# Rows of a mixed stage transposed in 32 x 32 blocks and stored feature by feature

## The chip, the cores and the metric

The kernel is one program on one core of a Trainium2 chip. Its time is that of the device in microseconds. The engines are TensorE (PE in the profile, its weight loads PEld), VectorE (DVE), ScalarE (ACT), GpSimd (POOL) and SyncE (SP). Every engine works through its own list of instructions in order. SP and ACT also issue DMAs here, and an ACT instruction that stands behind such an issue in the list waits for it.

## The reference

Two layers of a trunk with 256 context rows and 2048 latent rows of 1024 features. Each layer normalises the rows, projects them to 3040 columns, mixes them in three groups of heads and projects the 1024 mixed features back:

```python
y = concat([gated_head_norm(hg_lat, hg_norm_g, hgate),        # gated recurrence, 4 heads
            mla_lat.reshape(B, N, MLA_W) * silu(mgate),       # softmax attention, 4 heads of 128
            gated_head_norm(gla_lat, gla_norm_g, ggate)])     # linear attention, 4 heads
x_new = layer_norm(DEEPNORM_ALPHA * x + gate * (y @ w_out)) * ln_g + ln_b
```

All of it is 32-bit. Products of consequence are split into a high and a low part, so `y @ w_out` is three products (high x high, high x low, low x high).

## The kernel before

There are 18 tiles of 128 rows (2 of context, 16 latent), or 9 pairs of tiles. Each layer has three stages: `project`, `mix`, `output`.

In `mix` two generators are interleaved. `attention` takes one tile after the other and in each two pairs of heads (hp); for one of these it makes the scores (L905 to L909, evacuated by VectorE at L911), the exponential on ScalarE (L921), the transposes of the weights (`ptp`, L947), their split into high and low (`ph` by ScalarE at L79, `pl` by VectorE at L85), the weighted sums (`oc`, L934 and L939), their copy `os` (L963), the last product `poa` (L966) and the scaling into `ym` (L970). In all that is 34 tiles with 68 pairs of heads. `recurrence` walks over the 9 pairs of tiles, first backwards for states alone (`back_states`), then forwards (`recur`): six levels of gated products (`level_scores`, `pa` at L789) whose decays GpSimd multiplies up (tiles `t0` to `t5` at L725, keys and queries at L765), and at the end `chunk_outputs`, which copies the result to `o` (L822), squares it into a tile with the tag `t0` (L825), normalises and gates it on GpSimd (`rrs` L90, L831, L832). It is run 17 times, 9 in the first layer and 8 in the second, whose context is not needed.

Mixed rows go to the DRAM tensor `y` (2304 x 1024): 512 columns of a pair from `chunk_outputs` (L833, one store of 512 KB), 512 of a tile from `attend` (L973, one store of 256 KB), both from SP's queue. The `output` stage loads them by tile (L1074), transposes each of the 8 blocks of 128 x 128 on TensorE (L1081), splits the result out of PSUM (L79, L85) and multiplies it with `w_out` (L1101 to L1103, 48 products of 512 columns a tile).

The order of all instructions on each engine is set when the program is built: a scheduler plays the program through with its own costs and puts what is ready in line, with a bonus for some instructions (`high_priority`). Buffers (tag and `bufs`) bring in the waits. DMAs of both queues take their completion semaphores in turn from one set of eight (DMAHW0 to DMAHW7 in the order below); a DMA waits until the one that had its semaphore before has landed.

Of the kernel before, what the change touches and what calls it, by code (L numbers as in the profile page):

```python
# [7 lines left out]
F32 = mybir.dt.float32  # L8
# [3 lines left out]
ALU = mybir.AluOpType  # L12
# [4 lines left out]
P = 128  # L17
D = 1024
KD = D // P
# [35 lines left out]
class Trunk:  # L55
# [55 lines left out]
    def scratch(self, l):  # L111

        d, c, nt = self.dpool, self.cpool, self.nt
        S = {}
        S["scT"] = c.tile([P, KD, 2], F32, name=f"scT{l}")
        S["shT"] = c.tile([P, KD, 2], F32, name=f"shT{l}")
        S["gate"] = d.tile([2, D], F32, name=f"gate{l}")

        S["F"] = d.tile([P, self.npairs, 2, 3, SEG], F32, name=f"dF{l}")
        S["K"] = d.tile([P, self.npairs, 2, 3, SEG], F32, name=f"dK{l}")  # L120
        S["Q"] = d.tile([P, self.npairs, 3, SEG], F32, name=f"dQ{l}")
        S["nat"] = d.tile([nt, 1536], F32, name=f"dnat{l}")
# [508 lines left out]
    def pair_rows(self, nat, p, c0, c1):  # L631
        return nat[p * SEG:(p + 1) * SEG, c0:c1].rearrange("(j p) n -> p j n", p=P)

    def back_states(self, S, rp, rps):

        nc = self.nc
        st = rp.tile([P, 3, 64], F32, tag="sc", bufs=2, name="stc")
        nc.vector.memset(st, 0.0)
        L3 = 3 * SEG
        ncp = NCT // 2  # L640
        for p in list(range(ncp))[::-1] + list(range(ncp, self.npairs))[::-1]:
            f = rp.tile([P, 1 + L3], F32, tag="fa", name="bf")
            nc.gpsimd.memset(f[:, 0:1], 0.0)
            nc.sync.dma_start(out=f[:, 1:].rearrange("p (b n) -> p b n", b=3), in_=S["F"][:, p, 0])
            k = rp.tile([P, 3, SEG], F32, tag="ka", name="bk")
            nc.sync.dma_start(out=k, in_=S["K"][:, p, 0])
            vt = rp.tile([P, 2, 512], F32, tag="vg", name="bv")
            nc.sync.dma_start(out=vt, in_=self.pair_rows(S["nat"], p, 0, 512))
            pe = rp.tile([P, L3], F32, tag="qa", name="bpe")
            for b in range(3):  # L650
                bs = slice(b * SEG, (b + 1) * SEG)
                nc.vector.tensor_tensor_scan(pe[:, bs], f[:, bs], self.reset, 0.0, op0=ALU.mult, op1=ALU.max)
            tt = rp.tile([P, 3, NCH], F32, tag="btt", bufs=2, name="btt")
            last = [[SEG, 3], [64, NCH]]
            nc.vector.tensor_tensor(tt, view(pe[:], 63, last), view(f[:], 64, last), op=ALU.mult)
            kf = k.rearrange("p b n -> p (b n)")
            nc.gpsimd.tensor_tensor(kf, kf, pe, op=ALU.mult)
            pu = self.chunk_products(rp, rps, k, vt)

            sb = rp.tile([P, NCH, 3, 64], F32, tag="sbt", bufs=2, name="stb")  # L660
            nc.scalar.copy(sb[:, NCH - 1], st)
            for ch in range(NCH)[::-1]:
                to = sb[:, ch - 1] if ch else rp.tile([P, 3, 64], F32, tag="sc", bufs=2, name="stc")
                self.advance(to, sb[:, ch], tt, ch, pu)
            st = to
            nc.sync.dma_start(out=S["sb"][:, p], in_=sb)
            yield 1.0
# [129 lines left out]
    def chunk_outputs(self, S, rp, rps, p, acc, qa, qm, v2, vt, sbt, sts):  # L797
        nc = self.nc
        po = rps.tile([P, 2, 512], F32, tag="R", name="po")
        quads = ((0, 0), (1, 1), (1, 0), (0, 1))  # L800
        for j in range(2):
            for sl in range(4):
                for e, c in quads:
                    rows = slice(64 * e, 64 * e + 64)
                    o = 256 * j + 64 * sl
# [4 lines left out]
        for d, j in ((0, 0), (0, 1), (1, 0), (1, 1)):  # L810
            for sl in range(4):
                for e, c in quads:
                    rows = slice(64 * e, 64 * e + 64)
                    ch, b, o = 2 * j + c, min(sl, 2), 256 * j + 64 * sl
                    tk = slice(64 * ch, 64 * ch + 64)
                    q = qm[sl - 2][rows, d, tk] if sl > 1 else qa[rows, d, sl * SEG + 64 * ch:sl * SEG + 64 * ch + 64]
# [4 lines left out]
        o = rp.tile([P, 2, 512], F32, tag="acc", name="o")  # L821
        nc.scalar.copy(o.rearrange("p j (e n) -> p e j n", e=2), po.rearrange("p e (j n) -> p e j n", j=2))  # L822
        sq = rp.tile([P, 1024], F32, tag="t0", name="sq")
        of = o.rearrange("p j n -> p (j n)")
# [5 lines left out]
        o3 = of.rearrange("p (h d) -> p h d", d=64)  # L830
        nc.gpsimd.tensor_tensor(o3, o3, r.unsqueeze(2).to_broadcast([P, 16, 64]), op=ALU.mult)  # L831
        nc.gpsimd.tensor_tensor(o, o, vt[:, :, 512:1024], op=ALU.mult)  # L832
        nc.sync.dma_start(out=self.pair_rows(S["y"], p, 0, 512), in_=o)  # L833


    def query_group(self, S, ap, aps, t):
# [49 lines left out]
    def attend(self, S, K, ap, aps, G, t, j):  # L886
        nc = self.nc
# [2 lines left out]
        tk = slice(j * P, (j + 1) * P)  # L890
        mg = ap.tile([P, 512], F32, tag="mg", name="mg")
        nc.sync.dma_start(out=mg, in_=S["nat"][t * P:(t + 1) * P, 1024:1536])
        ym = ap.tile([P, 512], F32, tag="ym", name="ym")
        for hp in range(2):
            pexp, rinv = [], []
            for i in range(2):
                h = 2 * hp + i
                sx = ap.tile([P, self.nt], F32, tag="sx", bufs=3, name="sx")
                mx = ap.tile([P, 8], F32, tag="mx", bufs=2, name="mx")
                nb = 0  # L900
                for s in range(0, nk, 512):
                    n = min(512, nk - s)
                    pss = aps.tile([P, 512], F32, tag="s", bufs=2, name="pss")
                    ks = slice(s, s + n)
# [9 lines left out]
                nm = ap.tile([P, 1], F32, tag="nm", bufs=2, name="nm")  # L914
# [5 lines left out]
                sm = ap.tile([P, 1], F32, tag="sm", bufs=4, name="sm")  # L920
                nc.scalar.activation(sx[:, :nk], sx[:, :nk], AF.Exp, bias=nm, accum_out=sm)  # L921
                ri = ap.tile([P, 1], F32, tag="ri", bufs=4, name="ri")
# [19 lines left out]
            high, low = None, None  # L942
            for kc in range(0, nch, 2):
                pt = aps.tile([P, 2, 2, P], F32, tag="pt", bufs=2, name="ptp")
# [3 lines left out]
                ph = ap.tile([P, 2, 256], F32R, tag="ph", bufs=2, name="ph")  # L948
                pl = ap.tile([P, 2, 256], F32R, tag="pl", bufs=3, name="pl")
# [6 lines left out]
                low = (high[0], lastpl) if high is not None else None  # L956
# [7 lines left out]
            po = aps.tile([P, 2, P], F32, tag="mi", name="poa")  # L964
            for i in range(2):
                nc.tensor.matmul(po[:, i, :], os_[:, i * P:(i + 1) * P], S["uv"][:, 2 * hp + i, :],  # L966
                                 start=True, stop=True)
            for i in range(2):
                hs = slice((2 * hp + i) * P, (2 * hp + i + 1) * P)
                nc.vector.scalar_tensor_tensor(out=ym[:, hs], in0=po[:, i, :], scalar=rinv[i], in1=mg[:, hs],  # L970
                                               op0=ALU.mult, op1=ALU.mult)
            yield
        nc.sync.dma_start(out=S["y"][t * P:(t + 1) * P, 512:1024], in_=ym)  # L973

    def mix(self, l, S):

        nc = self.nc
        with ExitStack() as ctx:
            rp = self.pool(ctx)
            ap = Route(lambda: self.pool(ctx), "os mx nm sm ri", "mg", "ym", "ph pl", "cth ctl ks", "cq cqh cql",  # L980
                       "qn ropt ropa ropb", "rh rl", "qh ql", "gap", "cnh cnl", "sx")
            nc.gpsimd.memset(ap.tile([P, 16], F32, name="gap")[:, 0:1], 0.0)
            ps = Route(lambda: self.pool(ctx, psum=True), "mi", "R", "s", "oc", "pt")
            with self.tc.high_priority(offset=self.AHEAD):
                K = {nm: ap.tile([P, self.nt], F32R, name=nm) for nm in ("cth", "ctl", "ks", "cnh", "cnl")}
                src = (S["kT"][:, 0, :], S["kT"][:, 1, :], S["kN"].rearrange("p t n -> p (t n)"))
# [3 lines left out]
                for i in range(3):  # L990
                    if i == 1:
                        G = self.query_group(S, ap, ps, order[0])
                    for s in range(0, self.nt, 512):
                        n = min(512, self.nt - s)
                        ks = slice(s, s + n)
# [46 lines left out]
    def output(self, l, S):  # L1042
        nc, io = self.nc, self.io
        last = l == DEPTH - 1
        with ExitStack() as ctx:
            R = Route(lambda: self.pool(ctx), "yt", "woa", "sto mvo veo rso", "gate", "lng lnb", "z", "xto", "wob", "yhl")
            ps = Route(lambda: self.pool(ctx, psum=True), "low", "pz", "tr")
            nc.vector.memset(ps.tile([P, 512], F32, name="low")[:, 0:1], 0.0)
            gates = {}

# [8 lines left out]
            src = io["w_out"][l].rearrange("(k p) n -> p k n", p=P)  # L1059
            for k in range(KD):  # L1060
                w = R.tile([P, D], F32, tag="yt", bufs=2, name="woraw")
                nc.sync.dma_start(out=w, in_=src[:, k, :])
                for i, ws in enumerate((wh, wl)):
                    tag, n = ("woa", 11) if 2 * k + i < 11 else ("wob", 5)
# [5 lines left out]
            nc.sync.dma_start(out=lnb, in_=io["ln_b"][l:l + 1, :].to_broadcast([P, D]))  # L1070

            def turned(t):
                yt = R.tile([P, D], F32, tag="yt", bufs=2, name="yt")
                nc.sync.dma_start(out=yt, in_=S["y"][t * P:(t + 1) * P, :])  # L1074
                yhl = R.tile([P, 2, KD, P], F32R, tag="yhl", bufs=2, name="yhl")
                yh, yl = yhl[:, 0], yhl[:, 1]
                for q in range(2):
                    pt = ps.tile([P, 4, P], F32, tag="tr", bufs=2, name="pty")
                    for i in range(4):
                        k = 4 * q + i  # L1080
                        nc.tensor.transpose(pt[:, i, :], yt[:, k * P:(k + 1) * P], self.ident)  # L1081
                    self.split(yh[:, 4 * q:4 * q + 4, :], yl[:, 4 * q:4 * q + 4, :], pt)
                return yh, yl

            tiles = list(range(NCT if last else 0, self.ntiles))
# [1 line left out]
            for t in tiles:  # L1087
                yh, yl = nxt
# [8 lines left out]
                for n in range(2):  # L1097
                    cs = slice(n * 512, (n + 1) * 512)
                    pz = ps.tile([P, 512], F32, tag="pz", bufs=2, name="pzo")
                    for k in range(KD):  # L1100
# [5 lines left out]
                                                   op0=ALU.mult, op1=ALU.add)  # L1106
# [6 lines left out]
                dst = io["out"][0][(t - NCT) * P:(t - NCT + 1) * P, :] if last else self.xs_next[rows, :]  # L1113
# [112 lines left out]
```

## Time and profile before

| | |
|---|---|
| median of 2 runs | 3758.14 us (3754.92 to 3761.37) |
| the profiled execution | 3755.9 us, of which its span is 3754.2 us |
| busy: PE, DVE, ACT, POOL | 96%, 57%, 38%, 22% of the span |
| mix stages (not sharply bounded) | about 700 to 1724 us and 2600 to 3560 us |
| output stages | about 1724 to 1930 us and 3560 to 3754 us |
| TensorE clock granted | 0.986 of full speed |

"Busy" is the time in which an engine had an instruction under way; overlapping instructions are counted once. Matmuls overlap, so what one of them costs the queue is the distance between starts in a row, not its own duration. An idle engine costs something only where TensorE waits for it in the end.

### The profile page before, as it was taken

The page shows a single profiled execution, that of the slowest core. Times are in us where ns is not written, and L with a number is a line of the kernel's source. Part 1 is how long each engine was busy: PE and PEld are TensorE (multiplying, and loading weights), DVE is VectorE, ACT ScalarE, POOL GpSimd, SP SyncE. Part 2 cuts the span into 40 slices and gives each one's busy share as a digit, 9 for nine tenths or more (in the row PEclk, how much of TensorE's full clock was granted, in tenths as well). Part 3 has the DMA queues.
Part 4 walks back from the last instruction along what each step waited for, and adds up shares of the span by engine and source line. Part 5 has one row for each costly group of instructions (what it writes and reads, how often), then busy time and mean ns, then how long its engine had stood idle before and what let it go on. Part 6 is the DMA issues. An engine that isn't in the chain of part 4 may idle for free. (4 is left out here: it accounts for less than half of the span.)

```text
span 3754.2 us, 84546 instructions
## 1 busy us (share of the span) xinstructions
PE 3612.3 (96%) x36056; PEld 3264.7 (87%) x36056; DVE 2139.7 (57%) x5026; ACT 1435.5 (38%) x2296; POOL 811.6 (22%) x617
## 2 busy tenths in 40 slices
PE   8999999999999999998999999999999999999999
PEld 5899999888888888887879999998888888888787
DVE  6764242566666666656765442525665566656566
ACT  3525242344444444443115342523443444444400
POOL 1000000001335354341110000000022344644211
PEclk9999999999999999998999999999999999999999
DMA  7774344322122111116435443433221121221342
GB/s 253 234 202 145 126 132 143 111 81 91 49 69 84 56 61 62 55 43 206 153 110 170 146 152 108 154 120 113 83 90 43 60 68 57 78 78 44 102 143 101
DMA packets 263689, 410.79 MB, mean 109 GB/s; under 512 B 39633, under 2 KB 179985, under 8 KB 262289
## 3 DMA queue, kind: packets, MB, share of 16 engines
q1 hardware_dynamic: 261872, 403.04, 33.8%
q8 instruction: 283, 4.64, 0.5%
q10 hardware_dynamic: 1440, 2.36, 0.2%
q14 instruction: 94, 0.76, 0.1%
HBM read 288.66 MB, written 116.67 MB: 108 GB/s over the span
## 5 line engine op out<-in xcount | busy, mean ns | idle before, releaser
L421 PE MATMUL pj<-wh,hl 128*128 128x256 f32 (+1 forms) x2224 | 622.2, 280 | 7.9 <-DVE hl L85 7.9
L421 PE MATMUL pj<-wh,hh 128*128 128x256 f32 (+1 forms) x2224 | 623.9, 281 | 1.7 <-DVE ve L373 1.2
L421 PE MATMUL pj<-wl,hh 128*128 128x256 f32 (+1 forms) x2224 | 622.7, 280 | 0.1
L911 DVE TENSOR_SCALAR_CACHE_REDUCE sx<-pss 128x512 f32<-128x512 f32 (+1 forms) x648 | 402.9, 632 | 206.1 <-PE pss L909 181.7
L85 DVE TENSOR_TENSOR pl<-ptp,ph 128x512 fp32r<-128x512 f32 x580 | 389.5, 687 | 187.5 <-ACT ph L79 184.2
L79 ACT CAST ph<-ptp 128x512 fp32r<-128x512 f32 x580 | 327.9, 586 | 363.7 <-PE ptp L947 358.3
L421 PEld LDWEIGHTS pj<-wh,hl 128*128 128x128 f32 x2224 | 420.1, 189 | 8.7 <-DVE hl L85 8.6
L421 PEld LDWEIGHTS pj<-wh,hh 128*128 128x128 f32 x2224 | 421.1, 189 | 1.8 <-DVE ve L373 1.6
L421 PEld LDWEIGHTS pj<-wl,hh 128*128 128x128 f32 x2224 | 421.0, 189 | 0.6 <-issue 0.6
L947 PE MATMUL ptp<-ident,sx 128*128 128x128 f32 x2320 | 372.9, 279 | 25.4 <-DVE pl L85 15.8
L934 PE MATMUL oc<-ph,cnh 128*128 128x256 f32 x1160 | 339.6, 315 | 22.7 <-ACT ph L79 22.0
L921 ACT ACTIVATE sx<-sx,nm 128x2304 f32<-128x2304 f32 (+1 forms) x136 | 288.4, 2121 | 184.2 <-DVE nm L917 183.7
L432 PE MATMUL pj<-hh,wh 128*128 128x256 f32 x1136 | 317.3, 279 | 0.0
L947 PEld LDWEIGHTS ptp<-ident,sx 128*128 128x128 f32 x2320 | 273.2, 142 | 50.4 <-DVE pl L85 20.2
L432 PE MATMUL pj<-hh,wl 128*128 128x256 f32 x1136 | 316.2, 278 | 0.0
L432 PE MATMUL pj<-hl,wh 128*128 128x256 f32 x1136 | 315.8, 278 | 0.0
L934 PE MATMUL oc<-ph,cnl 128*128 128x256 f32 x1160 | 301.9, 283 | 0.0
L85 DVE TENSOR_TENSOR wl<-wraw,wh 128x1024 fp32r<-128x1024 f32 (+1 forms) x144 | 169.4, 1211 | 230.6 <-ACT wh L79 230.5
L905 PE MATMUL pss<-cth,qh 128*128 128x512 f32 (+1 forms) x648 | 264.9, 409 | 13.7 <-DVE sx L911 13.7
L934 PEld LDWEIGHTS oc<-ph,cnh 128*128 128x128 f32 x1160 | 222.1, 191 | 51.7 <-ACT ph L79 37.9
L939 PE MATMUL oc<-pl,cnh 128*128 128x256 f32 x1160 | 242.9, 291 | 0.0
L906 PE MATMUL pss<-ctl,qh 128*128 128x512 f32 (+1 forms) x648 | 242.9, 375 | 0.0
(253 smaller groups left out, 7888.0 us busy)
## 6 DMA issues: line engine op xcount, KB each, us to landing
wraw<-in_w_in_dram SPq DMA_DIRECT2D x132, 512.0 KB, 4.5
dnat<-stg SPq DMA_DIRECT2D x104, 256.0 KB, 2.1
vg<-dnat SPq DMA_DIRECT2D x17, 1024.0 KB, 6.1
yt<-dy SPq DMA_DIRECT2D x34, 512.0 KB, 3.6
wmt<-in_w_modT_dram SPq DMA_DIRECT2D x64, 256.0 KB, 4.0
fa<-dF SPq DMA_DIRECT2D x18, 768.0 KB, 4.5
ka<-dK SPq DMA_DIRECT2D x18, 768.0 KB, 4.2
dK<-stg SPq DMA_DIRECT2D x36, 256.0 KB, 4.6
```

What stands on the lines that cost most here:

```text
L79: nc.scalar.copy(hi, src)
L85: nc.vector.tensor_tensor(lo, src, hi, op=ALU.subtract)
L421: nc.tensor.matmul(pj[:, j, :n], h[pr][a][:, k, tk], w[b][:, k, :n], start=(k == 0 and a + b == 0), stop=(k == KD - 1 and a == 1))
L432: nc.tensor.matmul(pj[:, j, :], w[b][:, k, cs], h[pr][a][:, k, :], start=(k == 0 and a + b == 0), stop=(k == KD - 1 and b == 1))
L905: nc.tensor.matmul(pss[:, :n], G["qh"][hp][:, i, tk], K["cth"][:, ks], start=True, stop=False)
L906: nc.tensor.matmul(pss[:, :n], G["qh"][hp][:, i, tk], K["ctl"][:, ks], start=False, stop=False)
L911: nc.vector.tensor_scalar(sx[:, ks], pss[:, :n], SCALE, None, op0=ALU.mult, op1=ALU.max, accum_out=mx[:, nb:nb + 1])
L921: nc.scalar.activation(sx[:, :nk], sx[:, :nk], AF.Exp, bias=nm, accum_out=sm)
L934: nc.tensor.matmul(oc, K[k][:, keys(kc, c)], ph[:, c, :], start=(kc + c == 0 and k == "cnh"), stop=False)
L939: nc.tensor.matmul(oc, K["cnh"][:, keys(kc, c)], pl[:, c, :], start=False, stop=(kc + c == nch - 1))
L947: nc.tensor.transpose(pt[:, c, i, :], pexp[i][:, (kc + c) * P:(kc + c + 1) * P], self.ident)
```

## The change

The DRAM tensor becomes `yT`, features by rows (1024 x 2304). In `chunk_outputs` and `attend` VectorE transposes the finished tile in blocks of 32 x 32 (`ot`, 128 x 1024, with the tag `t0` that GpSimd's next level-0 decays use; `yo`, 128 x 256, one for each pair of heads). `put_turned` then writes it with one DMA for each 32 rows, from ScalarE's queue; its runs in DRAM are 32 numbers (128 bytes) long. So a pair of tiles takes 8 DMAs of 512 runs, a pair of heads 4 DMAs of 256 runs: 17 x 8 + 68 x 4 = 408 DMAs in place of 17 + 34 on SP's queue. `output` loads 128 features by 128 rows at a time (runs of 512 bytes, 1024 of them in a tile) and splits this tile directly, with no transposes and no PSUM tile.

```diff
+    def put_turned(self, S, src, f0, n, t0):
+        for a in range(4):
+            dst = S["yT"][f0:f0 + n, t0 + 32 * a:t0 + 32 * a + 32].rearrange("(b f) t -> f b t", f=32)
+            self.nc.scalar.dma_start(out=dst, in_=src[32 * a:32 * a + 32].rearrange("f (b t) -> f b t", t=32))
...
-        nc.sync.dma_start(out=self.pair_rows(S["y"], p, 0, 512), in_=o)
+        ot = rp.tile([P, 1024], F32, tag="t0", name="ot")
+        nc.vector.transpose(out=ot, in_=of)
+        for j in range(2):
+            self.put_turned(S, ot[:, 512 * j:512 * j + 512], 0, 512, (2 * p + j) * P)
...
+            yo = ap.tile([P, 256], F32, tag="yo", name="yo")
+            nc.vector.transpose(out=yo, in_=ym)
+            self.put_turned(S, yo, 512 + 256 * hp, 256, t * P)
             yield
-        nc.sync.dma_start(out=S["y"][t * P:(t + 1) * P, 512:1024], in_=ym)
...
-                yt = R.tile([P, D], F32, tag="yt", bufs=2, name="yt")
-                nc.sync.dma_start(out=yt, in_=S["y"][t * P:(t + 1) * P, :])
+                yt = R.tile([P, KD, P], F32, tag="yt", bufs=2, name="yt")
+                nc.sync.dma_start(out=yt, in_=S["yT"].rearrange("(k p) t -> p k t", p=P)[:, :, t * P:(t + 1) * P])
...
-                    pt = ps.tile([P, 4, P], F32, tag="tr", bufs=2, name="pty")
-                    for i in range(4):
-                        k = 4 * q + i
-                        nc.tensor.transpose(pt[:, i, :], yt[:, k * P:(k + 1) * P], self.ident)
-                    self.split(yh[:, 4 * q:4 * q + 4, :], yl[:, 4 * q:4 * q + 4, :], pt)
+                    ks = slice(4 * q, 4 * q + 4)
+                    self.split(yh[:, ks, :], yl[:, ks, :], yt[:, ks, :])
```

Three places show what the scheduler made of it. The first is ScalarE around the second copy `os` of the first mix stage, with the stores of one pair of heads. Before:

```order
L963 COPY os<-oc 128x256
L921 ACTIVATE sx,sm<-sx,nm 128x2304
L611 COPY kn<-pk 128x384
L79 CAST ph<-ptp 128x512 x2
L611 COPY kn<-pk 128x384
```

Now:

```order
L971 COPY os<-oc 128x256
L638 DMA dy_95<-yo 32x8x32 x4
L611 COPY kn<-pk 128x384
L929 ACTIVATE sx,sm<-sx,nm 128x2304
L611 COPY kn<-pk 128x384
```

Four stores and a copy stand between `os` and the exponential that followed it at once. On TensorE the first transposes of that exponential's result (`ptp`, a row of 6) came after 20 score products of 512 columns behind `poa`; now they come after 25, one group of 256 columns and the products `pu`.

The second is ScalarE around the 14th `os`, with the stores of the first pair of tiles and of a pair of heads. Before:

```order
L963 COPY os<-oc 128x256
L921 ACTIVATE sx,sm<-sx,nm 128x2304
L79 CAST qh<-pq 128x512
L79 CAST ph<-ptp 128x512 x2
L791 COPY acc<-pa 128x1024
```

Now:

```order
L971 COPY os<-oc 128x256
L638 DMA dy_95<-ot 32x16x32 x8
L638 DMA dy_95<-yo 32x8x32 x4
L797 COPY acc<-pa 128x1024
L79 CAST qh<-pq 128x512
L929 ACTIVATE sx,sm<-sx,nm 128x2304 x2
```

Twelve stores, the copy `acc` and a cast stand ahead of the exponentials. On TensorE seven groups of scores, 24 products `pq` and the 32 products `pa` of level 0 now stand between `poa` and the 6 `ptp`, and the `pa` of level 1 come right behind these.

The third is GpSimd at the same place, with what each instruction waits for. `t_12141` and `t_12235` are the level-0 decays `t0` of the next pair. Before:

```order
L725 TENSOR_TENSOR t_12141<-fa 128x768 [waits DVE_49]
L90 TENSOR_TENSOR rrs<-rss,mhalf 128x16 [waits DVE_49]
L725 TENSOR_TENSOR t_12182<-t_12141 128x384 [waits Pool_49]
L831 TENSOR_TENSOR o<-o,rrs 128x1024 [waits Pool_49]
L765 TENSOR_TENSOR ka<-ka,t_12141 128x192x2x2 [waits Activation_49]
```

Now:

```order
L90 TENSOR_TENSOR rrs<-rss,mhalf 128x16 [waits DVE_49]
L837 TENSOR_TENSOR o<-o,rrs 128x1024 [waits Activation_49,Pool_49]
L838 TENSOR_TENSOR o<-o,vg 128x1024 [waits DMAHW2_49,Pool_49]
L731 TENSOR_TENSOR t_12235<-fa 128x768 [waits DMAHW3_49,DMAHW4_49,DMAHW2_49,DMAHW6_49,DMAHW1_49,DMAHW7_49,DMAHW0_49,DVE_49]
L771 TENSOR_TENSOR ka<-ka,t_12235 128x192x2x2 [waits Activation_49,Pool_49]
```

The decays stood ahead of the normalisation; now they stand behind it and wait for VectorE and for the landing of the stores from `ot`, whose buffer they take.

## Rows read from the trace of the kernel before

**Rows 1.** The page: busy us (share of the span) and instructions by engine.
```profile
PE 3612.3 (96%) x36056; PEld 3264.7 (87%) x36056; DVE 2139.7 (57%) x5026; ACT 1435.5 (38%) x2296; POOL 811.6 (22%) x617
```

**Rows 2.** Stretches: us, busy us of PE, PEld, DVE, ACT, POOL; clock, DMA share, GB/s.
```profile
700.00:1724.00 1024.00, 971.77 (x12019) 850.94 (x12018) 647.08 (x1697) 458.25 (x717) 366.55 (x258) 0.98 0.24 75
1724.00:1930.00 206.00, 199.00 (x964) 163.96 (x963) 141.50 (x227) 32.80 (x60) 24.35 (x21) 0.97 0.45 160
2600.00:3560.00 960.00, 924.99 (x11114) 807.17 (x11114) 601.40 (x1574) 431.67 (x663) 331.60 (x235) 0.99 0.22 68
```

**Rows 3.** Timeline of PE: start, us, operation, shapes, count [idle before <-releaser].
```profile
3548.27 1.09 PE L1081 MATMUL pty<-ident,yt 128*128 128x128 f32 x8 [0.54 <-DMA yt<-dy]
```

**Rows 4.** DMA issues: count, KB each, median us to landing.
```profile
v<-dnat SPq DMA_DIRECT2D x34, 256.0 KB, 4.1
...
dy<-ym SPq DMA_DIRECT2D x34, 256.0 KB, 2.1
```

**Rows 5.** Issue on the queue by line: count, ns min/median/max, first and last start.
```profile
L833 SPq DMA_DIRECT2D dy<-o x17: 359/370/526, 1039.3 to 3508.9; - x17
...
L693 SPq DMA_DIRECT2D v<-dnat x34: 579/613/1862, 703.4 to 3428.4; - x34
...
L997 ACTq DMA_DIRECT2D kraw<-dkT x10: 326/326/338, 557.6 to 2436.9; - x10
...
L194 SPq DMA_DIRECT2D gate<-mc x2: 378/734/1089, 111.2 to 111.6; - x2
```

**Rows 6.** Line L194's landings, and all packets from 241.5 to 254 us.
```profile
DMA to landing us min/median/max: 12.5/12.6/12.8
...
DMA packets 1618, 0.57 MB, mean 46 GB/s; under 512 B 1228, under 2 KB 1490, under 8 KB 1618
```

**Rows 7.** Waits: who for whom, us in total, times, longest.
```profile
ACT sx L921 <- DVE nm L917: 183.7, 100, 4.8
```

**Rows 8.** DVE by line and shape: busy us, mean ns | idle before <-releaser.
```profile
L793 DVE COPY_PREDICATED acc<-mask,pa 128x1024 f32<-128x1024 uint8 x102 | 137.0, 1343 | 73.8 <-PE pa L789 67.1 <-issue 5.7
...
L375 DVE TENSOR_SCALAR xt<-xt,mv,rs 128x1024 f32<-128x1024 f32 x36 | 29.1, 809 | 11.6 <-POOL rs L90 11.6
```

**Rows 9.** Timelines of ACT, DVE and PE around the second `os`.
```profile
772.63 0.37 ACT L963 COPY os<-oc 128x256 f32<-128x256 f32 x1 [3.58 <-PE oc L939]
774.71 2.22 ACT L921 ACTIVATE sx<-sx,nm 128x2304 f32<-128x2304 f32 x1 [1.70 <-DVE nm L917]
776.92 0.46 ACT L611 COPY kn<-pk 128x384 f32<-128x384 f32 x1
...
773.81 0.61 DVE L970 SCALAR_TENSOR_TENSOR ym<-poa,ri,mg 128x128 f32<-128x128 f32 x2
...
773.13 0.64 PE L966 MATMUL poa<-uv,os 128*128 128x128 f32 x4
773.53 0.48 PE L905 MATMUL pss<-cth,qh 128*128 128x512 f32 x1
...
778.53 0.82 PE L947 MATMUL ptp<-ident,sx 128*128 128x128 f32 x6
```

**Rows 10.** Timelines of POOL, DVE, ACT and PE around the 14th `os`.
```profile
1026.72 1.47 POOL L725 TENSOR_TENSOR t<-fa 128x768 f32<-128x768 f32 x1
1028.14 2.91 POOL L90 TENSOR_TENSOR rrs<-rss,mhalf 128x16 f32<-128x16 f32 x1
...
1034.23 2.22 POOL L765 TENSOR_TENSOR ka<-ka,t 128x768 f32<-128x768 f32 x1 [0.52 <-ACT km L755]
...
1036.87 2.39 POOL L832 TENSOR_TENSOR o<-o,vg 128x1024 f32<-128x1024 f32 x1
...
1051.53 2.36 POOL L765 TENSOR_TENSOR qa<-qa,fa 128x384 f32<-128x384 f32 x2 [11.31 <-PE pa L789]
...
1045.08 1.03 ACT L791 COPY acc<-pa 128x1024 f32<-128x1024 f32 x1
...
1037.09 0.64 PE L966 MATMUL poa<-uv,os 128*128 128x128 f32 x4
1043.53 0.82 PE L947 MATMUL ptp<-ident,sx 128*128 128x128 f32 x6
```

More of the change, by code (lines that the diff above doesn't have):

```diff
@@ L126, in scratch @@
         S["sb"] = d.tile([P, self.npairs, NCH, 3, 64], F32, name=f"dsb{l}")
-        S["y"] = d.tile([nt, D], F32, name=f"dy{l}")
+        S["yT"] = d.tile([D, nt], F32, name=f"dy{l}")
         return S
@@ L892, in attend @@
         nc.sync.dma_start(out=mg, in_=S["nat"][t * P:(t + 1) * P, 1024:1536])
-        ym = ap.tile([P, 512], F32, tag="ym", name="ym")
         for hp in range(2):
@@ L967, in attend @@
                                  start=True, stop=True)
+            ym = ap.tile([P, 256], F32, tag="ym", name="ym")
             for i in range(2):
                 hs = slice((2 * hp + i) * P, (2 * hp + i + 1) * P)
-                nc.vector.scalar_tensor_tensor(out=ym[:, hs], in0=po[:, i, :], scalar=rinv[i], in1=mg[:, hs],
-                                               op0=ALU.mult, op1=ALU.mult)
+                nc.vector.scalar_tensor_tensor(out=ym[:, i * P:(i + 1) * P], in0=po[:, i, :], scalar=rinv[i],
+                                               in1=mg[:, hs], op0=ALU.mult, op1=ALU.mult)
+            yo = ap.tile([P, 256], F32, tag="yo", name="yo")
+            nc.vector.transpose(out=yo, in_=ym)
+            self.put_turned(S, yo, 512 + 256 * hp, 256, t * P)
             yield
-        nc.sync.dma_start(out=S["y"][t * P:(t + 1) * P, 512:1024], in_=ym)
     def mix(self, l, S):
@@ L979, in mix @@
             rp = self.pool(ctx)
-            ap = Route(lambda: self.pool(ctx), "os mx nm sm ri", "mg", "ym", "ph pl", "cth ctl ks", "cq cqh cql",
+            ap = Route(lambda: self.pool(ctx), "os mx nm sm ri", "mg", "ym yo", "ph pl", "cth ctl ks", "cq cqh cql",
                        "qn ropt ropa ropb", "rh rl", "qh ql", "gap", "cnh cnl", "sx")
@@ L1046, in output @@
             R = Route(lambda: self.pool(ctx), "yt", "woa", "sto mvo veo rso", "gate", "lng lnb", "z", "xto", "wob", "yhl")
-            ps = Route(lambda: self.pool(ctx, psum=True), "low", "pz", "tr")
+            ps = Route(lambda: self.pool(ctx, psum=True), "low", "pz")
             nc.vector.memset(ps.tile([P, 512], F32, name="low")[:, 0:1], 0.0)
```

## The prediction

> **What bounds the kernel.** I read the page first, then a table of stretches, then the waits, then timelines of two places in the mix stage. The page shows TensorE busy for 3612 of 3754.2 us [rows 1], so all its idle time is 142 us. The stretches say the same of each stage: in the two mix stages TensorE idles 52 of 1024 and 35 of 960 us, while ScalarE has 458 and 432 us of work there; in the first output stage it idles 7 of 206 us [rows 2]. So time is won only by work taken from TensorE's list, and lost by whatever makes its list wait. The waits show how ScalarE lies beside it: a hundred times it waited for VectorE ahead of an exponential, 184 us in all, 1.8 us each [rows 7]. That is slack, but little of it at a time.
>
> **Taken away.** TensorE loses 34 x 8 = 272 transposes. A row of eight takes 1.09 us [rows 3]; with some 0.27 us for the last one to drain that is 0.117 us of the queue for each. 272 x 0.117 = 32 us, all of it on the path, since in the output stages TensorE waits for next to nothing. That stage then has 48 products a tile; VectorE has 141 of 206 us there [rows 2], so nothing else takes over. SP loses 51 stores and the waits ahead of them; no wait of TensorE hung on them: 0.
>
> **Added and hidden.** VectorE transposes 17 x [128 x 1024] and 68 x [128 x 256]. The trace has no such operation. Others over 1024 numbers take 0.81 to 1.34 us [rows 8]; I take 1.2, and 0.4 for the small one (two operations of 128 columns took 0.61 us [rows 9]). That is 48 us beside 1248 us of work in 1984 us: hidden, except where a chain below runs through it. The split reads SBUF now: 0, hidden by the products of the tile before. The loads of `yt` become 1024 runs of 512 bytes; they are issued a tile ahead, more than 10 us: 0.
>
> **Added on ScalarE's list.** 408 issues. On that queue an issue of a plain pattern took 0.33 us; on SP the old store of `o` took 0.37 and the load `v`, with 64 partitions, 0.61 [rows 5]. The new stores have 32 partitions and three dimensions. I take 0.5, between 0.36 and 0.61: 204 us (147 to 249) on an engine with 890 us of work in 1984. There is room, so the question is what stands behind each burst.
>
> One pair of heads (51 of the 68 stand without an `ot` burst). From the start of `poa`, T: `ym` ends at T+1.3 [rows 9], the small transpose at about T+1.9, four issues at T+3.3 to T+4.3, `kn` 0.46, the exponential 2.2 and its sum 0.2: T+6.2 to T+7.2. Before, the exponential began 1.6 us after T and its transposes came at T+5.4. The new order puts about 7.6 us of products between (25 score products at the 0.23 us of the rows, one group at half, the rest 1.2 us), so `ptp` stands at T+7.8: covered, with about 1 us over. But this work was taken from places where it covered other waits. Lower bound 0, upper bound 1 us; I take 0.5: 25 us.
>
> A pair of tiles (17). `o` is ready by 1034, ahead of `poa` at 1037.1 = T, because `t0` and the decays no longer stand between [rows 10]. VectorE transposes it by T+1.9. Eight issues end at T+4.8 to T+6.8, four more at T+6.2 to T+9.2, `acc` 1.0 [rows 10], a cast 0.6, the exponential 2.4: T+10.2 to T+13.2. TensorE reaches `ptp` at about T+11.5 (seven groups 7.5, `pq` 2.8, `pa` 0.7): a stall of 0 to 1.7 us. **The longer chain is GpSimd's.** `t0` must wait until the last store from `ot` has landed, 2.1 to 4.1 us after its issue if it goes like the stores and loads of [rows 4]: T+6.9 to T+10.9. Then `t0` 1.5, keys 2.2, queries 2.4 [rows 10], about 6.1 us: T+13 to T+17. The `pa` of level 1 stand at T+12.2 in TensorE's list, so it waits 1 to 5 us. Together 1 to 5.4 us a pair of tiles. Which end it is hangs on how fast runs of 128 bytes go out: 512 in a store are 32 for each of 16 engines. If a run took 25 ns, a store took 0.8 us, the eighth landed at about T+10.4, and the wait was 4.3. I take 4: 68 us. Nothing in the trace excludes that the new order gains a little elsewhere; I put it at 0.
>
> SP's loads take semaphores from the same eight, so after a burst of twelve the next ones wait for its landing, up to some 4 us. They fill buffers a stage ahead: 0, and counted in the upper bounds.
>
> **Sum.** -32 + 25 + 68 = +61 us on the profiled execution's 3755.9 us (span 3754.2 and 1.7 around it): 3817. The median of the two runs is 2.2 us higher, which makes **3819 us**, 1.6% above. A measurement of this kernel tells about 2% (75 us) from no change, so this is "within 2%", close to its edge.
>
> **The rivals.**
>
> *The cover holds.* The scheduler put work ahead of each place where TensorE would have waited. If its costs fit, all stalls are at their lower bounds (17 x 1 us or less) and the 32 us stay: 3726 to 3745. For it: TensorE idles only 87 us in both mix stages now, under the same scheduler. Against it: GpSimd's new wait. Chance 0.16.
>
> *The bursts at their upper bounds.* 17 x 5.4 + 51 x 1 - 32 = +111: about 3869 (3833 to 3900). It decides from 4.9 us a pair of tiles at 0.5 a pair of heads. Chance 0.23.
>
> *Short runs jam the memory.* The only stores of short runs in the trace are 4 bytes long: 1024 of them landed after 12.5 us, and in a stretch of 12.5 us after another such store the queues moved 0.57 MB, though they had more to do [rows 6]. That is 195 ns a run for each engine. If runs of 128 bytes took 50 ns, a store would take 1.6 us, the eighth would land at T+16.7 and level 1 wait until T+22.8, 10.6 us late: 17 x 10.6 + 25 - 32 = +173, 3931. At 100 ns it is 12.8 us more for each, +391, 4149. Against it: the 4-byte runs all fall into the same few kilobytes, these do not, and a store of rows lands in 2.1 us [rows 4]. It makes the kernel slower by more than 2% from about 30 ns a run. Chance 0.20.
>
> The Trainium skill (DMA: Bandwidth & Descriptors, Specifications) gives 512 bytes as the least transfer at full rate; below it the engine reads, modifies and writes. By that rule this rival is the forecast. The trace agrees for 4 bytes, by the 12.5 us above; for 128 bytes no row shows it.
>
> *The transposes cost more than their distance.* One lasts 0.27 us from start to end. If that whole time fell away, 272 x 0.27 = 73 us less, and stalls near 0 would make it 3685, faster by just 2%. Against it: the row of eight in 1.09 us. Chance 0.03. The Trainium skill (VectorE: DVE Perf Modes, The three transpose paths) puts a transpose of 128 x 128 on TensorE at 390 ns, for a 16-bit type. By that the gain would be 106 us, an estimate from that page; the row of eight disagrees, and the sum goes by the row.
>
> That the change does not do what it says (loads of `yt` that wait for all stores, for instance) has no chance of its own: in the new order the first products of the output stage still stand ahead of the last `poa`.
>
> **Numbers.** Forecast 0.38 (3780 to 3833), cover 0.16, bursts 0.23, jam 0.20, more than the distance 0.03. Faster 0.03; within 2%, 0.38 + 0.16 = 0.54; slower 0.23 + 0.20 = 0.43. The range goes from 3724, the cover with nothing lost, to 3940, the jam at 50 ns; outside lie the 0.03 and about half of the jam, 0.13 in all.
>
> **What the profile of the changed kernel would show.** Right: no `pty`; ScalarE's queue with 408 more issues of 0.36 to 0.61 us; output stages some 16 us shorter each; GpSimd's `t0` waiting for stores from `ot`, and TensorE idle ahead of `pa` by 1 to 5 us once a pair of tiles; stores from `ot` landing in under 5 us. Wrong: TensorE idle ahead of `ptp` or the scores in every pair of heads (the price of the small burst is off), landings of 8 us and more (the jam), or mix stages no longer than before (the cover).

## The result, and the profile after

The changed kernel takes 3860.7 us (median of 2 runs, 3860.15 to 3861.26) against 3758.14: ratio 1.029, 95% interval 1.0268 to 1.0312. It is slower by 2.9%. Differences below are given in us as the ratio's distance from 1 times 3750, since the kernel before stood between 3748 and 3758 us beside the different runs: the change is +109 by that measure.

The page after, busy time by engine; its span is 3858.4 us [rows 1]:

```profile
PE 3633.9 (94%) x35784; PEld 3256.4 (84%) x35784; DVE 2168.5 (56%) x5111; ACT 1438.9 (37%) x2296; POOL 811.0 (21%) x617
```

The 272 transposes are gone from TensorE's count. Its idle time rose from 142 to 224.5 us, and its busy time rose too, by 21.6 us. Nobody else became the bound: VectorE got 29 us more, ScalarE 3. By stage (columns as in [rows 2]; the stages now end later, and the third window lies as far behind the last projection product and ahead of the last `poa` as the third of [rows 2], since these moved from 2568.8 to 2626.7 and from 3562.5 to 3670.5 us):

```profile
700.00:1785.00 1085.00, 995.97 (x12009) 855.88 (x12008) 660.01 (x1738) 456.39 (x714) 365.57 (x258) 0.98 0.26 71
1785.00:1990.00 205.00, 190.39 (x869) 155.56 (x869) 143.85 (x231) 35.77 (x64) 26.72 (x21) 0.95 0.50 161
2658.00:3668.00 1010.00, 949.25 (x11105) 819.93 (x11106) 614.54 (x1611) 433.24 (x664) 330.54 (x235) 0.98 0.24 65
```

The two mixes grew by about 61 and 50 us, and TensorE idles 89 and 61 us in them (52 and 35 before). In some 205 us of the first output stage it now does 869 instructions instead of 964, at 0.95 of the clock. From the last `poa` to the last product an output stage takes 211 us instead of 216 and 179 instead of 183.

What TensorE waited for, before and now (who for whom, us, times, longest):

```profile
PE oc L934 <- ACT ph L79: 22.0, 40, 1.8
PE ptp L947 <- ACT sx L921: 8.9, 6, 3.8
PE pzo L1101 <- DVE z L1104: 6.0, 1, 6.0
PE pa L789 <- POOL qa L765: 1.3, 3, 0.7
```

```profile
PE oc L942 <- ACT ph L79: 43.2, 47, 4.1
PE ptp L955 <- ACT sx L929: 24.2, 11, 9.0
PE pzo L1109 <- DVE z L1112: 24.2, 2, 14.2
PE pa L795 <- POOL qa L771: 9.0, 13, 2.0
```

What ScalarE makes late, the casts `ph` and the exponential `sx`, costs most. The products of the output stages (`pzo`) wait for VectorE, which still works off the mix. GpSimd's late queries are a small row.

The new stores on ScalarE's queue (count, ns min/median/max of one issue) [rows 5]:

```profile
L638 ACTq DMA_DIRECT2D dy<-yo x272: 309/462/1624, 750.5 to 3674.3; - x136
L638 ACTq DMA_DIRECT2D dy<-ot x136: 309/520/3125, 1049.6 to 3610.6; - x136
```

Their landings (KB each, median us) [rows 4]:

```profile
dy<-yo ACTq DMA_DIRECT2D x272, 32.0 KB, 1.7
dy<-ot ACTq DMA_DIRECT2D x136, 64.0 KB, 4.4
```

The new transposes on VectorE [rows 8]:

```profile
L982 DVE STREAM_TRANSPOSE yo<-ym x68: 401/445/456, 750.1 to 3671.4; 128x256 f32<-128x256 f32 x68
L840 DVE STREAM_TRANSPOSE ot<-o x17: 1234/1245/1247, 1048.3 to 3605.7; 128x1024 f32<-128x1024 f32 x17
```

Durations are as foretold. Now the waits (who for whom, us, times, longest) of ScalarE and GpSimd [rows 7]:

```profile
ACT sx L929 <- DVE nm L925: 86.0, 52, 6.5
ACT kn L611 <- DMA dy<-yo: 77.1, 16, 6.8
ACT acc L797 <- DMA dy<-ot: 59.2, 7, 11.0
ACT acc L797 <- DMA dy<-yo: 37.4, 4, 9.8
ACT sx L929 <- DMA dy<-yo: 26.7, 7, 10.4
...
POOL t L731 <- DMA dy<-yo: 96.5, 10, 10.7
POOL t L731 <- DMA dy<-ot: 41.2, 4, 11.5
```

A wait of ScalarE "for" a store here is its own list: the instruction stands behind the issues. With four smaller rows that are not shown these come to 241 us at 42 places; ScalarE's old slack ahead of the exponential went from 184 to 86 us. GpSimd's first product of a pair (`t0`, L731) waits 138 us at 14 places.

One such place, the end of a pair of tiles (timelines of ACT, POOL and PE: start, us, operation [idle before <-releaser]) [rows 10]:

```profile
1395.78 0.37 ACT L971 COPY os<-oc 128x256 f32<-128x256 f32 x1 [3.59 <-PE oc L947]
1397.43 5.17 ACTq L638 DMA_DIRECT2D dy<-ot  x8
1402.70 1.98 ACTq L638 DMA_DIRECT2D dy<-yo  x4
1404.72 1.01 ACT L797 COPY acc<-pa 128x1024 f32<-128x1024 f32 x1 [8.57 <-DMA dy<-yo]
1405.63 2.22 ACT L929 ACTIVATE sx<-sx,nm 128x2304 f32<-128x2304 f32 x1
...
1392.96 2.40 POOL L838 TENSOR_TENSOR o<-o,vg 128x1024 f32<-128x1024 f32 x1
1404.89 1.47 POOL L731 TENSOR_TENSOR t<-fa 128x768 f32<-128x768 f32 x1 [9.54 <-DMA dy<-yo]
...
1405.79 2.35 PE L795 MATMUL pa<-qa,km 64*64 64x64 f32 x64 [0.90 <-ACT acc L797]
1408.07 0.44 PE L955 MATMUL ptp<-ident,sx 128*128 128x128 f32 x2
```

From 1397.4 to 1404.7 ScalarE does nothing but issue twelve stores. The copy `acc`, which frees the PSUM tile of `pa`, and the exponential that TensorE's next transposes need both stand behind them; GpSimd starts 2.3 us after the last of the eight `ot` issues. TensorE lives on products in hand until 1404.9 and then thins out: busy 3.16 of the 5 us after 1405, 3.51 of the next 5, with the clock at 0.59 (between 1.2 and 2.4 GHz) where it had been at 1.00:

```profile
1405.00:1410.00 5.00, 3.16 (x70) 2.69 (x70) 1.49 (x2) 5.00 (x5) 4.92 (x4) 1.00 0.05 10
1410.00:1415.00 5.00, 3.51 (x52) 3.17 (x56) 1.45 (x3) 1.92 (x6) 4.70 (x7) 0.59 0.46 136
1415.00:1420.00 5.00, 5.00 (x67) 4.65 (x60) 2.72 (x3) 2.10 (x4) 3.83 (x2) 0.72 0.06 24
```

The small burst at the place of [rows 9] does no harm:

```profile
776.55 0.64 PE L974 MATMUL poa<-uv,os 128*128 128x128 f32 x4
784.89 0.81 PE L955 MATMUL ptp<-ident,sx 128*128 128x128 f32 x6
...
777.87 0.45 DVE L982 STREAM_TRANSPOSE yo<-ym 128x256 f32<-128x256 f32 x1
778.35 1.82 ACTq L638 DMA_DIRECT2D dy<-yo  x4
780.21 0.48 ACT L611 COPY kn<-pk 128x384 f32<-128x384 f32 x1 [3.79 <-DVE sx L919]
780.59 2.22 ACT L929 ACTIVATE sx<-sx,nm 128x2304 f32<-128x2304 f32 x1
```

The exponential ends 6.3 us after `poa` began, `ptp` comes at 8.3, with no idle time ahead of it.

### The profile page after: what moved, and what is told of

It reads as the page before. It is cut to its first block, busy times and chain, and to the rows that moved or that the text cites. A ratio compares the mean times of both kernels' runs of the same rounds, so it can differ in the third digit from the quotient of the medians.

```text
span 3858.4 us, 84719 instructions
## 1 busy us (share of the span) xinstructions
PE 3633.9 (94%) x35784; PEld 3256.4 (84%) x35784; DVE 2168.5 (56%) x5111; ACT 1438.9 (37%) x2296; POOL 811.0 (21%) x617
## 3 DMA queue, kind: packets, MB, share of 16 engines
q10 hardware_dynamic: 147232, 20.21, 3.1%
## 5 line engine op out<-in xcount | busy, mean ns | idle before, releaser
L955 PE MATMUL ptp<-ident,sx 128*128 128x128 f32 x2320 | 372.0, 280 | 48.3 <-ACT sx L929 24.2
L942 PE MATMUL oc<-ph,cnh 128*128 128x256 f32 x1160 | 341.9, 318 | 44.8 <-ACT ph L79 43.2
L795 PEld LDWEIGHTS pa<-qa,km 64*64 64x64 f32 (+1 forms) x6528 | 191.2, 139 | 62.5 <-issue 17.2
```

The lines of the kernel that those rows point to most:

```text
L795: nc.tensor.matmul(out, w, mv, start=True, stop=True, tile_position=pos)
L942: nc.tensor.matmul(oc, K[k][:, keys(kc, c)], ph[:, c, :], start=(kc + c == 0 and k == "cnh"), stop=False)
L955: nc.tensor.transpose(pt[:, c, i, :], pexp[i][:, (kc + c) * P:(kc + c + 1) * P], self.ident)
```

## The experiments

Each ratio is to the kernel before, run beside it; us as above. The scheduler lines up the instructions of each version anew, so an edit brings its own order along: behind the 14th `os`, for example, ScalarE's list in e3 has `acc`, an exponential and `qh`, where the change has twelve stores, `acc`, `qh` and two exponentials. No run holds the order fixed, so each difference is that of an edit together with its order.

| run | median us | ratio (95%) | us |
|---|---|---|---|
| the change | 3860.7 | 1.0290 (1.0268 to 1.0312) | +109 |
| e1_output_only | 3733.6 | 0.9964 (0.9952 to 0.9975) | -14 |
| e2_mix_only | 3882.1 | 1.0362 (1.0340 to 1.0384) | +136 |
| e3_sp_queue | 3769.3 | 1.0060 (1.0043 to 1.0078) | +22 |
| e4_long_runs | 3840.3 | 1.0253 (1.0232 to 1.0274) | +95 |
| e5_long_one | 3810.8 | 1.0160 (1.0144 to 1.0176) | +60 |
| e6_own_ot | 3844.1 | 1.0242 (1.0227 to 1.0257) | +91 |
| e7_sp_long | 3782.5 | 1.0080 (1.0063 to 1.0097) | +30 |
| e8_block_load | 3765.4 | 1.0026 (1.0013 to 1.0039) | +10 |
| e9_output_clean | 3733.1 | 0.9951 (0.9934 to 0.9968) | -18 |
| e10_turns_clean | 3775.2 | 1.0054 (1.0038 to 1.0071) | +20 |
| e11_block_load4 | 3726.0 | 0.9921 (0.9902 to 0.9940) | -30 |
| e12_turns_own | 3745.2 | 0.9989 (0.9979 to 0.9999) | -4 |

### Which half, and which queue

**e1_output_only**

> The output stages alone: the mix stores rows as the kernel before does (one SyncE store for a pair of tiles, one for a tile, 2 KB runs, no VectorE transposes), into the memory that the output stages then read as if it were turned, so the values are those of other places. My prediction put -32 us on this part (272 transposes by 0.117 us): 3726 us, ratio 0.991. If the spare transposes were hidden behind something else, or TensorE's clock eats the gain, 3745 to 3760; if each cost its latency, 3685. If the whole loss of the change lies in the mix, this kernel plus the loss of the mix alone must add up to the changed kernel (+102.6 us).

```diff
+    def ynat(self, S, h):
+        a, n = S["yT"][:, :], self.nt - S["off"]
+        return bass.AP(a.tensor, a.offset + 512 * h * n, [[512, n], [1, 512]])
...
-        nc.vector.transpose(out=ot, in_=of)
-        for j in range(2):
-            self.put_turned(S, ot[:, 512 * j:512 * j + 512], 0, 512, (2 * p + j) * P)
+        nc.sync.dma_start(out=self.ynat(S, 0)[p * SEG - S["off"]:(p + 1) * SEG - S["off"]].rearrange("(j p) n -> p j n", p=P), in_=o)
```

-14 us. But the trace shows TensorE waiting 26.6 us (2 times) ahead of `pzo` for tile loads that could start only after the last store, which the change itself does not have. So the run doesn't settle the size; e9 was made for that.

**e2_mix_only**

> The mix of the changed kernel (VectorE transposes, 408 stores from ScalarE's queue, 128-byte runs), with TensorE's transposes back in the output stages, which read the same memory as natural rows. If the sum holds with -32 us for the output stages: 3860.7 + 32 = 3893 us (ratio 1.036). If the output stages gained nothing: 3861. If the turned loads of the output stages, not the mix, made the loss: 3760 to 3790.

```diff
-                nc.sync.dma_start(out=yt, in_=S["yT"].rearrange("(k p) t -> p k t", p=P)[:, :, t * P:(t + 1) * P])
+                for h in range(2):
+                    nc.sync.dma_start(out=yt[:, 512 * h:512 * h + 512], in_=self.ynat(S, h)[t * P - S["off"]:(t + 1) * P - S["off"]])
...
+                        nc.tensor.transpose(pt[:, i, :], yt[:, k * P:(k + 1) * P], self.ident)
```

The output stages are those of the kernel before, reading `yT`'s memory as rows; the values they read belong to other places. +136: the whole loss is in the mix. Against the change the spare transposes are worth 27 us here.

**e3_sp_queue**

> The same 408 stores issued from SyncE instead of ScalarE; all else as in the changed kernel. Theory 1 (ScalarE's list is held by the bursts of issues, 408 times about 0.5 us and their waits, and what it owes TensorE comes late): most of the loss goes, 3735 to 3790. Theory 2 (the buffer that GpSimd shares with ot comes free only when the last store has landed): little changes, 3840 to 3865. Theory 3 (128-byte runs hold up the DMA engines or the memory for everybody): unchanged, 3850 to 3870. A rival against moving them: SyncE's loads stand behind the stores and come late, 3870 to 3950.

```diff
-            self.nc.scalar.dma_start(out=dst, in_=src[32 * a:32 * a + 32].rearrange("f (b t) -> f b t", t=32))
+            self.nc.sync.dma_start(out=dst, in_=src[32 * a:32 * a + 32].rearrange("f (b t) -> f b t", t=32))
```

+22, so one word takes away 86 of 109 us. The page's line by engine, and the stores' issue by SP:

```profile
PE 3598.6 (96%) x35784; PEld 3237.5 (86%) x35784; DVE 2166.5 (58%) x5111; ACT 1438.3 (38%) x2296; POOL 811.2 (22%) x617
```

```profile
L638 SPq DMA_DIRECT2D dy<-yo x272: 302/443/2147, 750.3 to 3586.2; - x136
L638 SPq DMA_DIRECT2D dy<-ot x136: 303/499/2266, 1037.3 to 3532.4; - x136
```

An issue costs SP as much as ScalarE (0.44 and 0.50 us), but nobody computes there: TensorE's idle time falls from 224.5 to 168.8 us (3767.4 - 3598.6), its busy time by 35 us. Theory 1 holds for most of the loss. The Trainium skill (DMA: Bandwidth & Descriptors, Rules for kernel authors) says that spreading DMAs over queues saves only the sequencer's issue time; here taking the 408 issues off ScalarE's list was worth 86 us.

**e4_long_runs**

> As many stores (408), from ScalarE's queue, with the same bytes and the same 32 partitions each, but every row of a partition is one run of 1 or 2 KB at its natural place (so the values land elsewhere); 8 to 16 times fewer pieces. Theory 1 with a price that does not hang on the pieces: 3850 to 3870. Theory 3, or theory 1 with an issue whose price hangs on the pieces: 3740 to 3800. Theory 2: the landings of ot get shorter with fewer pieces, so 3800 to 3840.

```diff
-            dst = S["yT"][f0:f0 + n, t0 + 32 * a:t0 + 32 * a + 32].rearrange("(b f) t -> f b t", f=32)
-            self.nc.scalar.dma_start(out=dst, in_=src[32 * a:32 * a + 32].rearrange("f (b t) -> f b t", t=32))
+            dst = self.ynat(S, f0 // 512)[t0 - S["off"] + 32 * a:t0 - S["off"] + 32 * a + 32, f0 % 512:f0 % 512 + n]
+            self.nc.scalar.dma_start(out=dst, in_=src[32 * a:32 * a + 32])
```

+95, that is 14 less than the change; the intervals touch. `ot` stores land after 3.5 us instead of 4.4. But e4 has the flaw of e1 too: TensorE waits 17.3 us ahead of `pzo` for tile loads, while its wait for `z` there is 9.4 us, against 24.2 in the change. How much of the 17 us is lost is not settled, so the short runs are worth 14 to some 31 us on ScalarE's queue: a small part either way.

**e5_long_one**

> ScalarE's queue again, natural places as in the run with long runs, but one store of 128 partitions for each yo (68) and two for each ot (34): 102 issues instead of 408, the same bytes, the same VectorE transposes and waits. Theory 1a (each issue's own time holds ScalarE's list, about 0.5 us each): of the 71 us between the 408 long-run stores on ScalarE (3840) and SyncE's version (3769) a quarter stays, 3770 to 3795. Theory 1b (ScalarE's list is held by what the first store of a burst waits for, VectorE's transpose or an old landing, which one store waits for as well): 3820 to 3845.

```diff
+        self.nc.scalar.dma_start(out=self.ynat(S, f0 // 512)[t0 - S["off"]:t0 - S["off"] + P, f0 % 512:f0 % 512 + n], in_=src)
```

+60, 35 less than e4 (both with the 17.3 us ahead of `pzo`) for 306 issues less, about 0.11 us each. Neither band was hit: it fell between 1a and 1b. ScalarE's waits behind stores are down to 9 us, but `t0` waits longer than in e7, where SP issues the same stores (109.1 us, 13 times, against 77.2, 11 times; `ot` lands after 6.2 us against 5.5), so e5 minus e7 is no clean price of an issue.

### The buffer and VectorE's transposes

**e6_own_ot**

> The changed kernel, with ot in the buffer of v2 (read for the last time by TensorE just before, and filled for the next pair of tiles by a SyncE load that has the whole pair's time) instead of that of t0 and sq, so that GpSimd's first product of the next pair no longer waits for the last landing of an ot store. Theory 2 (that wait is the larger term, as my prediction had it: 17 times 4 us = 68 us): 3780 to 3815. Theory 1 (ScalarE's list, whose own next instructions are as late): 3840 to 3865. A rival: SyncE's queue now waits for the landing and the loads behind it come late, 3860 to 3880.

```diff
-        ot = rp.tile([P, 1024], F32, tag="t0", name="ot")
+        ot = rp.tile([P, NCH, 256], F32, tag="v2", name="ot").rearrange("p c n -> p (c n)")
```

+91, 18 less than the change. All waits of `t0` for stores are gone, 138 us of them, and one eighth of that came back. With ScalarE's list held, `acc` and the exponential are late anyway.

**e7_sp_long**

> The VectorE transposes of the changed kernel, with 102 natural stores from SyncE: the mix of before plus 85 transposes, and output stages without TensorE's. Theory 4 (VectorE's 68 times 0.45 and 17 times 1.25 us, about 52 us, lie on the path): 3760 to 3790. My prediction's term (hidden): as the output stages alone, 3730 to 3745.

```diff
-        self.nc.scalar.dma_start(out=self.ynat(S, f0 // 512)[t0 - S["off"]:t0 - S["off"] + P, f0 % 512:f0 % 512 + n], in_=src)
+        self.nc.sync.dma_start(out=self.ynat(S, f0 // 512)[t0 - S["off"]:t0 - S["off"] + P, f0 % 512:f0 % 512 + n], in_=src)
```

The minus line is that of e5. +30; in it TensorE waited 16.2 us for a first tile load, the flaw of e1, so e10 repeats it without.

**e9_output_clean**

> The output stages alone again, without what disturbed the first such run (there each output stage began with 11 to 16 us in which TensorE waited for a tile load that could not start before the last store of the mix): the mix and its stores are the kernel before's, and the output stages load tiles in the changed kernel's pattern (8 runs of 512 bytes to a partition) from a tensor written long before, so their values are others'. My prediction's term: -32 us. From the first run, -13.5 and the 26.6 us of those waits taken off: -40. If the spare transposes were covered: 0 to -15.

```diff
-                nc.sync.dma_start(out=yt, in_=S["yT"].rearrange("(k p) t -> p k t", p=P)[:, :, t * P:(t + 1) * P])
+                nc.sync.dma_start(out=yt, in_=view(S["F"][:, 0, 0, 0, :], t * P, [[12 * P, KD], [1, P]]))
```

The minus line is that of the change; all else is the kernel before, without TensorE's transposes. -18 us (-12 to -25), less than both numbers expected, though TensorE's busy time fell by 24.9 us (to 3587.4). In each output stage `pzo` waits once for VectorE's `z`, 16.1 us in all, against 6.0 before: the products now start while VectorE still works off the mix (the change waits 24.2 us there). That this wait holds the rest of the 32 us is read from the trace, not tested by itself; e11, which has no such wait, gains 30.

**e10_turns_clean**

> As the last, with the VectorE transposes of the changed kernel in the mix, and 102 stores of whole tiles from SyncE (2 and 1 KB runs, natural places); against the last run it shows what the 85 transposes and the waits tied to them cost without ScalarE's queue and without short runs. Theory 4 (VectorE's time, 52 us, lies on the path in the mix): 40 to 55 us above the last run. My prediction (hidden): 0 to 10 us above it. Between: part of them, where a softmax waits behind them on VectorE.

To the load of e9 comes, in `put_turned`:

```diff
+        self.nc.sync.dma_start(out=S["y"][t0:t0 + P, f0:f0 + n], in_=src)
```

+20, so 39 above e9, at the edge of theory 4's band. But its waits name another cause:

```profile
POOL t L729 <- DMA dy<-ot: 76.6, 11, 8.4
PE pa L793 <- POOL qa L769: 22.8, 17, 4.4
ACT acc L795 <- DVE ot L838: 24.6, 12, 4.6
```

`t0` waits for the landing of the `ot` stores, GpSimd's queries come late and `pa` waits for them: the chain of my prediction, seen without ScalarE's bursts.

**e12_turns_own**

> The run with the turns alone (85 VectorE transposes, stores of whole tiles from SyncE, 1.0054), and ot in v2's buffer, as in the run on the changed kernel: GpSimd's first product of a pair of tiles no longer waits for the landing of the store of ot (76.6 us of such waits in the profile of the turns alone, which TensorE sees as waits of pa for qa), while VectorE does the same 52 us of transposes at the same places. Theory 2: most of the 39 us between the turns alone (1.0054) and the output stages alone (0.9951) goes, 0.996 to 0.999. Theory 4 (VectorE's own time on the path): 1.004 to 1.006.

The edit is that of e6, made in e10. -4: of the 39 us 24 went with the buffer, and 14 (4 to 24) are left for all of VectorE's 51 us and the waits tied to it. `t0` no longer waits for any store, and:

```profile
PE pa L793 <- POOL qa L769: 1.0, 2, 0.7
ACT acc L795 <- DVE ot L838: 7.8, 7, 3.1
```

Theory 2 explains most of e10, theory 4 a small rest. Without e12 the 39 us would have been put down to VectorE, because 51 us of transposes look like so good a fit.

The buffer also sets GpSimd's order. In the change, e3 and e10 the next pair's decays stand behind the normalisation at all 15 places where a next pair follows; in e6 and e12 they stand ahead of it again, as before. The first such place in e12:

```profile
1021.54 1.46 POOL L729 TENSOR_TENSOR t<-fa 128x768 f32<-128x768 f32 x1
1022.97 2.90 POOL L90 TENSOR_TENSOR rrs<-rss,mhalf 128x16 f32<-128x16 f32 x1
```

So the 24 us are the price of the shared buffer, the later place in the list and the wait for the landing together; the runs do not part the two.

### A version that beats both

**e8_block_load**

> A version pointed to by these runs: the mix exactly as before (natural stores by SyncE, no transposes there), and the turning in the output stages: each tile's rows are loaded in four crosswise pieces (SyncE, 1 KB runs, 32 partitions each; the order of features over K chunks is another, and w_out's rows are loaded in the same order), VectorE transposes 32x32 blocks once per tile (1.25 us, 34 tiles, 42 us in all) and no TensorE transposes. Nothing is stored in short runs and ScalarE's list holds nothing more. If VectorE's transposes hide in the output stages: 3730 to 3740. If they come before the products of z on VectorE and TensorE waits: up to 42 us more, 3740 to 3780.

```diff
+                for q in range(4):
+                    nc.sync.dma_start(out=yb[32 * q:32 * q + 32].rearrange("u a k f -> u a (k f)"),
+                                      in_=S["y"][t * P:(t + 1) * P, 256 * q:256 * q + 256].rearrange("(a u) n -> u a n", u=32))
+                yt = R.tile([P, 4, KD, 32], F32, tag="ytt", name="yt")
+                nc.vector.transpose(out=yt.rearrange("p a k u -> p (a k u)"), in_=yb.rearrange("p a k f -> p (a k f)"))
...
-            src = io["w_out"][l].rearrange("(k p) n -> p k n", p=P)
+            src = io["w_out"][l].rearrange("(q k f) n -> k q f n", q=4, f=32)
```

+10, no gain, and the cause was neither of the two expected: the end of the mix grew, since ScalarE waited 47.8 us for the new loads of `w_out` (`woraw`; 11.8 us before) with a softmax in line behind.

**e11_block_load4**

> The version that turns tiles in the output stages, with w_out's rows loaded by four plain loads of 32 rows to a chunk instead of one load over rows in four places. In the run before this one the six loads of w_out at the end of a mix were issued over 30 us, in the kernel before over 18, and ScalarE, which copies them, held the last softmax back. If that was its loss: 3705 to 3735. If the loss is VectorE's 34 transposes in the output stages: 3750 to 3770 as there.

```diff
-                nc.sync.dma_start(out=w, in_=src[k])
+                for q in range(4):
+                    nc.sync.dma_start(out=w[32 * q:32 * q + 32], in_=src[k, q])
```

The minus line is that of e8. -30 us (-22 to -37): 0.8% faster than the kernel before and 3.6% faster than the change, the fastest kernel here. Who waited for the loads of `w_out`, in e8 and in e11, and the first output stage of e11:

```profile
  ACT wo L79: 47.8, 14
```

```profile
  ACT wo L79: 23.5, 13
```

```profile
1724.00:1930.00 206.00, 204.48 (x936) 167.27 (x936) 167.37 (x260) 33.60 (x61) 29.21 (x23) 0.99 0.51 161
```

VectorE turns the 34 tiles in the output stages (1.23 us each) and still has 39 us to spare in this stretch, while TensorE idles 1.5 us (7 before).

## Why the prediction was right in part

The range held the time; the likeliest case, "within 2%", did not come. The sum of the runs, each part against its neighbour: outputs -18 (e9), `ot` in `t0`'s buffer +24 (e10 to e12), VectorE and the rest of the new chain +14 (e12 to e9), short runs, 306 more stores on SP and tile loads that again depend on the stores +2 (e10 to e3), ScalarE's queue +86 (e3 to the change): +108. Mine was +61.

- **Bound and stages**: right that TensorE's list decides; no other engine became the bound. But of the 104 us that the span grew 83 are idle time and 22 busy time, where the sum had 32 us less of it. Busy time that grows behind stalls was a term that it did not have.
- **-32 us for the transposes**: the mechanism right, the size too large for this order of work: -18 in e9, -27 between e2 and the change, -30 in e11. The distance in a row is nearer than the whole duration; the output stages did not get 16 us shorter each in the change but 5 and 4, and in them TensorE waits 24.2 us for `z` amid the mix's leftovers. The rival "the transposes cost more than their distance" is refuted: no run gives 73 us. The Trainium skill's 390 ns (VectorE: DVE Perf Modes, The three transpose paths), given for a 16-bit type, would be 106 us, an estimate; the measurement decides against it here: 18 to 30 us by 272 are 0.07 to 0.11 us each.
- **VectorE's transposes hidden**: durations right (1.245 and 0.445 us for 1.2 and 0.4 taken), the 0 nearly right: some 14 us (4 to 24) with the waits tied to them, of which `acc` waiting for `ot` is the part that the trace names.
- **`yt` loads and SP at 0**: right. Loads land after 4.6 us and held ScalarE 5.6 us in all.
- **+25 us for the bursts on ScalarE**: this step failed. The price of an issue was right (0.46 and 0.52 us for 0.5), and the burst that I followed ran as I wrote. What failed is "51 of the 68 stand without an `ot` burst", priced by one exponential at one place: behind a burst stand whatever copies the scheduler put there (`kn`, `acc`, `km`, `rh`), each holding a PSUM tile or an operand of TensorE, and beside `ot` twelve issues make one block of 7 us. ScalarE stood behind stores for 241 us at 42 places, and TensorE waited 43.2 us for `ph` and 24.2 for `sx` (22.0 and 8.9 before). Without the stores on its list 86 us go, and TensorE's busy time alone is 35 us shorter: beyond my upper bound of 51 for this term, and beyond 80 with the 1.7 us that I allowed ScalarE in each pair of tiles.
- **+68 us for a pair of tiles**: the chain right (`t0` waits for the landing, `pa` of level 1 for GpSimd), the size not: 24 us with the stores on SP, 18 on ScalarE, so 1.1 to 1.4 us a pair and not 4. `t0` waited 9.8 us at each of 14 places, no longer than the chain had it (10 to 14, from `o` 3.1 us ahead of T to T+6.9 and T+10.9). What failed is that 4 us of it reach TensorE each time: most was GpSimd's slack, and TensorE waited for `qa` 9.0 us in all, at 13 places. That this error and the one on ScalarE pull opposite ways was luck, and it, not the sizes, kept the sum near.
- **Rivals**: the time lies where "the bursts at their upper bounds" put it (3833 to 3900), but by ScalarE's list, not by 5.4 us of GpSimd's a pair. "The cover holds" is refuted. "Short runs jam the memory" too: 14 to some 31 us on ScalarE's queue (e4), about 2 on SP's, stores landing after 1.7 and 4.4 us. The Trainium skill's 512 bytes (DMA: Bandwidth & Descriptors, Specifications) may hold for a transfer's rate: the same 20.21 MB took the DMA engines 3.1% of their time in short runs and 1.8% in long ones. At these amounts the kernel's time hardly hung on it.

## What to carry to other kernels

An engine that is 38% busy may still have no room for 200 us of DMA issues: ask what stands behind each burst in its list, above all copies that free PSUM, and put stores on a queue that computes nothing. A wait's length in a view is not its price: here 138 us of waits were worth 18. Give the waiter another buffer and time it, and look whether the order of instructions moved along. Before putting a loss down to the work that was added, take away the wait that came with it.

## What the runs showed of the hardware

- **128-byte pieces were cheap.** ScalarE's queue after, and in e4 with long runs (packets, MB, share of 16 engines):

```profile
q10 hardware_dynamic: 147232, 20.21, 3.1%
```

```profile
q10 hardware_dynamic: 21024, 20.21, 1.8%
```

  That is 3.1% of 16 x 3858 us over 147232 packets, some 13 ns each, half of the 25 ns on which my wait of 4.3 us rested. The 195 ns that I had worked out for 4-byte pieces [rows 6] is another measure: it came from a landing, and packets of 4 bytes took 9 ns each in the change's trace.
- **One load over rows in four places was slow.** `woraw` (512 KB) held ScalarE 47.8 us as one load with the rows in four blocks of 32, and 23.5 as four loads of 32 rows. What in such a load is slow stays open.
- **Stalls cost busy time too.** With 272 transposes gone TensorE's busy time rose by 21.6 us (in e9 the same removal took 24.9 off). 19 us of it are the same 6528 products of `pa` (210.6 us before):

```profile
L795 PE MATMUL pa<-qa,km 64*64 64x64 f32 (+1 forms) x6528 | 229.6, 234 | 14.9 <-POOL qa L771 9.0 <-ACT acc L797 5.7
```

  Part of that is the clock: its mean fell from 0.986 to 0.980, and it fell right behind stalls as at 1410 us above. Of these products 474 lasted over 300 ns (32 before; the median is 218 in both) and took 24.1 us of busy time instead of 1.1. At the 0.032 us each that these products took before, 474 would be 15 us, so some 9 of the 19 us go with the clock. How the rest divides was not tested.
